# A block's closing steps as a chain of their own beside the next block's row fetches

## The chip, the cores and the metric

The kernel runs on one core of one Trainium2 chip. The time is device microseconds of an execution; the kernel before took 3956.99 us, the median of 3 runs (3949.39 to 3957.73). The profiled execution took 3962.2 us, with a span of 3960.4 us from its first to its last instruction.

## What is computed

One layer of an encoder on 1024 tokens of width 1024: adaLN, a token mixer (attention and a two-way state space model, merged by gates), and then PEER, a channel mixer that picks 128 of 16384 experts for each token. The change lies in the last lines, for the tokens 0 to 383:

```python
def one(xt):                                   # peer, for a block of tokens
    ...                                        # top-k of product keys: idx [T, 8, 16], gates g
    u = u_tab[idx]
    a = jax.nn.gelu(jnp.einsum('thkd,td->thk', u, xt))
    vv = v_tab[idx]
    return jnp.einsum('thk,thkd->td', g * a, vv)
...
x = x + g2[:, None, :] * peer(h, ...)
return rmsnorm(x, final_norm_w)
```

## The kernel before

PEER is done in two ways. **Fetched rows.** For the tokens 0 to 383, three blocks of 128, the rows of `u_tab` and `v_tab` are fetched by index. **Dense.** For the other 640 tokens every expert is computed: the hidden activations of all 16384 experts (`parked_part`, products of three passes at L209 to L211 into the banks `hb`, each followed by a write of the activations `a` to `a_d`), the gates of the chosen experts placed into a dense matrix by one-hot products (`quad` L1478, weighted on GpSimd L1484, products `place` L1493 into a bank, copies to the staging buffers `stg` L1496, in pairs of two 2048 KB writes to `G_d`, L1625), and then, by groups of three experts' rows, `Wh` and `Wl` (L1689, L1692), the splits of `v` (L179, L180), products into banks and `acc` adds on VectorE (L1722). Hidden parts and placement share a stage; the groups, with what is left of the hidden parts, are the dense end behind it.

The fetches run beside that. `fetched()` is a generator; for each block it makes 128 row fetches of `u` (`rows`, L1282: an indirect DMA of GpSimd, one row of 1024 values for each of 128 tokens, into one of ten buffers `br`), and for each of them one row product on VectorE (`dot`, L1314) with the token rows, which `begin` (L1309) has copied into the PSUM tile `gx`. Then come the weights (gelu times gate, transposed), 128 fetches of `v`, and matmuls that sum the rows into `gx` (`add`, L1361). `gx` has two banks and one buffer, so the token rows of the next block, the sums of this one and all that the end below puts there take turns.

The end of a block is `finish` and `final`: copy `gx` to `bacc` (L1369), eight transposes back into `gx` (L1374), load of the residual x1 into the same `bacc` buffer (L1247), eight adds on VectorE (L1252), eight squares on ScalarE (L1260) with sums on PE (L216) into `gx`, the root (`rstd`, L228), its broadcast by PE into `gx` (L237), eight multiplies by the norm's weight (L1271) and the store (L1272). `yield "w"` cuts it into steps.

What sets the order: a planner that keeps three clocks, `at_pe`, `at_dve` and `at_dma`. After each piece of the dense work `feed` (L1503) steps the generator as long as the clock of the DMA lags, 1.6 us for each row; a step that yields "w" ends the round. The instructions of VectorE and GpSimd, and the order of the matmuls in the first stage, are those in which the code is written out; in the dense end PE, ScalarE and SyncE are arranged by the scheduler.

Other single banks come from `P1()`: three `pb` and, behind the placement, `io` as a fourth. The raw weights (`wr`), staging writes, activation writes and the x1 loads all stand in SyncE's queue.

## Time and profile before

| | |
|---|---|
| median of 3 runs | 3956.99 us (3949.39 to 3957.73) |
| profiled execution | 3962.2 us, span 3960.4 us |
| PE (TensorE matmul), busy | 92% |
| PEld (TensorE weight load) | 81% |
| DVE (VectorE) | 65% |
| POOL (GpSimd) | 46% |
| ACT (ScalarE) | 34% |
| DMA, mean over the span | 215 GB/s |
| mean granted clock of TensorE | 0.963 |

A share is a mean over stages. In the span the hidden parts' products begin at 1393 us, the placement's run from 2054 to 2490 us, and the first `Wh` of the dense end is made at 2523 us. The three blocks of fetched rows end at about 2240, 3020 and 3720 us; block 0 ends within the placement, blocks 1 and 2 in the dense end. "SPq" is SyncE's queue of DMA issues. In a timeline the bracket behind a row is the idle time of the engine just before it and what ended it. The clock is given as a share of 2.4 GHz.

### The profile page before, as it was taken

How to read it: one execution, taken by the hardware profiler on the slowest of the kernel's cores; microseconds unless marked ns; L12 is line 12 of the kernel's file. 1: busy time of each engine (PE TensorE's matmuls, PEld its weight loads, DVE VectorE, ACT ScalarE, POOL GpSimd, SP SyncE). 2: the span in 40 equal slices, each digit the busy share in tenths (PEclk: the TensorE clock that was granted, in tenths of full speed). 3: DMA queues.
4: the chain of work that ended last, by engine and by line, in shares of the span. 5: the costliest groups of instructions: out<-in, count | busy, mean ns of one | idle time of the engine just before them, and what ended most of it. 6: DMA issues, size and time to landing. Idle time of an engine off the chain costs nothing. (4 is left out here: it accounts for less than half of the span.)

```text
span 3960.4 us, 61117 instructions
## 1 busy us (share of the span) xinstructions
PE 3631.6 (92%) x22927; PEld 3189.8 (81%) x22927; DVE 2574.5 (65%) x5289; ACT 1356.3 (34%) x2672; POOL 1803.3 (46%) x1526
## 2 busy tenths in 40 slices
PE   7999999988889899999889798699999999999998
PEld 4777767766679799987678698697888999888997
DVE  5788831457672678787875567594447898545556
ACT  5455532223323433322236465222122222222222
POOL 3111122566454567778775456444443444444200
PEclk9999999998899999999999899799999999999999
DMA  5111134233375258877767778888887888888632
GB/s 197 47 46 48 55 117 144 92 106 101 122 241 168 94 201 317 311 284 258 244 231 273 264 265 320 310 300 303 322 323 246 295 297 292 310 317 314 236 117 81
DMA packets 387064, 852.32 MB, mean 215 GB/s; under 512 B 32720, under 2 KB 146896, under 8 KB 384080
## 3 DMA queue, kind: packets, MB, share of 16 engines
q1 hardware_dynamic: 276176, 445.72, 32.9%
q0 software_dynamic: 110592, 402.70, 28.7%
q8 instruction: 180, 2.95, 0.3%
q14 instruction: 116, 0.95, 0.1%
HBM read 739.70 MB, written 108.59 MB: 214 GB/s over the span
## 5 line engine op out<-in xcount | busy, mean ns | idle before, releaser
L209 PE MATMUL hb<-ah,wh 128*128 128x320 f32 x2048 | 653.2, 319 | 24.0 <-ACT a L1459 24.0
L211 PE MATMUL hb<-ah,wl 128*128 128x320 f32 x2048 | 641.1, 313 | 9.7 <-POOL wl L199 9.7
L210 PE MATMUL hb<-al,wh 128*128 128x320 f32 x2048 | 639.9, 312 | 0.0
L1282 POOL DMA_INDIRECT br<-u,bidx x384 | 370.3, 964 | 369.0 <-DVE br L1314 243.2
L199 POOL TENSOR_TENSOR wl<-wr,wh 128x512 fp32r<-128x512 f32 x269 | 352.9, 1317 | 397.3 <-ACT wh L198 367.6
L209 PE MATMUL pb<-Wh,vh 128*128 128x320 f32 x1536 | 477.1, 317 | 57.1 <-ACT Wh L1689 33.7
L180 POOL TENSOR_TENSOR wl<-wr,wh 128x512 fp32r<-128x512 f32 x172 | 233.0, 1358 | 615.5 <-ACT wh L179 450.6
L1282 POOL DMA_INDIRECT br<-v,ixt x384 | 376.8, 981 | 267.5 <-PE gx L1361 155.1
L210 PE MATMUL pb<-Wl,vh 128*128 128x320 f32 x1536 | 481.4, 314 | 1.7 <-DVE Wl L1692 1.6
L211 PE MATMUL pb<-Wh,vl 128*128 128x320 f32 x1536 | 479.6, 313 | 0.0
L1314 DVE SCALAR_TENSOR_TENSOR br<-br,gx 128x1024 f32<-128x1024 f32 x384 | 454.0, 1214 | 8.6 <-DMA br<-u,bidx 6.3
L209 PEld LDWEIGHTS hb<-ah,wh 128*128 128x128 f32 x2048 | 391.9, 191 | 52.7 <-ACT a L1459 28.2
L211 PEld LDWEIGHTS hb<-ah,wl 128*128 128x128 f32 x2048 | 390.7, 191 | 11.3 <-POOL wl L199 10.3
L210 PEld LDWEIGHTS hb<-al,wh 128*128 128x128 f32 x2048 | 391.5, 191 | 0.0
L1722 DVE TENSOR_TENSOR acc<-acc,pb 128x320 f32<-128x320 f32 x491 | 230.6, 485 | 222.2 <-PE pb L211 221.0
L179 ACT CAST vh<-vr 128x512 fp32r<-128x512 f32 x256 | 151.1, 618 | 649.8 <-PE pb L210 449.0
L209 PEld LDWEIGHTS pb<-Wh,vh 128*128 128x128 f32 x1536 | 289.6, 190 | 84.4 <-ACT Wh L1689 37.0
L198 ACT CAST wh<-wr 128x512 fp32r<-128x512 f32 x288 | 178.2, 619 | 397.8 <-PE hb L210 188.2
L210 PEld LDWEIGHTS pb<-Wl,vh 128*128 128x128 f32 x1536 | 292.5, 190 | 5.4 <-DVE Wl L1692 4.3
L211 PEld LDWEIGHTS pb<-Wh,vl 128*128 128x128 f32 x1536 | 292.9, 191 | 0.4
L1478 DVE TENSOR_TENSOR quad<-io,rig 128x1024 f32<-128x1024 f32 x160 | 191.7, 1221 | 139.1 <-PE pb L1493 78.0
L180 DVE TENSOR_TENSOR vl<-vr,vh 128x512 fp32r<-128x512 f32 x256 | 203.9, 797 | 76.8 <-ACT vh L179 76.8
(367 smaller groups left out, 8218.4 us busy)
## 6 DMA issues: line engine op xcount, KB each, us to landing
wr<-uT SPq DMA_DIRECT2D x256, 256.0 KB, 3.9
vr<-v SPq DMA_DIRECT2D x256, 256.0 KB, 5.3
G_d<-stg SPq DMA_DIRECT2D x20, 2048.0 KB, 11.7
gt<-G_d SPq DMA_DIRECT2D x42, 960.0 KB, 6.5
a_d<-a SPq DMA_DIRECT2D x85, 320.0 KB, 5.3
a<-a_d SPq DMA_DIRECT2D x85, 320.0 KB, 5.9
wr<-wi SPq DMA_DIRECT2D x84, 256.0 KB, 2.7
sq<-adaT SPq DMA_DIRECT2D x32, 512.0 KB, 3.8
```

What stands on the lines that cost most here:

```text
L179: ACT.copy(hi, src)
L180: (eng or POOL).tensor_tensor(lo, src, f32(hi), op=OP.subtract)
L198: ACT.copy(h, raw)
L199: late.append(lambda: (eng or POOL).tensor_tensor(w, raw, f32(h), op=OP.subtract))
L209: PE.matmul(o, lhsT=wh, rhs=xh, start=first, stop=False)
L210: PE.matmul(o, lhsT=wh, rhs=xl, start=False, stop=False)
L211: PE.matmul(o, lhsT=wl, rhs=xh, start=False, stop=last)
L1282: POOL.indirect_dma_start(out=r, out_offset=None, in_=A[tab], in_offset=bass.IndirectOffsetOnAxis(ap=idx, axis=0))
L1314: V.scalar_tensor_tensor(v2(r), v2(r), 1.0, hrow[0], op0=OP.mult, op1=OP.mult, accum_out=a[:, s:s + 1])
L1478: V.tensor_tensor(x, iota.unsqueeze(1).unsqueeze(1).to_broadcast([128, 2, 4, 128]), ig[:, 0:2, t:t + 4].unsqueeze(3).to_broadcast([128, 2, ...
L1722: V.tensor_tensor(acc[:, m, js], acc[:, m, js], o, op=OP.add)
```

## The change

The residual, its norm and the store are no longer written out as steps of the generator with "w" between. `finish` copies `gx` to `bacc`, starts the load of the first half of x1, and leaves a generator `tail` behind, with five pieces. `go_on()` runs one piece after every third `u` fetch of the next block; what is left at the end runs in a loop at the end of `fetched`. A piece of the residual makes four transposes into one single bank, four adds in place into `bacc`, and, in the first piece, issues the load of the second half. The halves of x1 share one buffer `bx1` of [128, 4, 128], and the two passes of squares, of [128, 512] each, use it too. Sums and broadcast go to single banks; the norm is made in place. `ba`, the row products' sums, has one buffer instead of two. Lines behind the change are 4 higher (L1314 is L1318, L1282 is L1286, L1484 is L1488, L1722 is L1726), those behind `go_on` more (L1369, the copy, is L1374).

```diff
--- before.py
+++ after.py
@@ -1235,41 +1235,45 @@
         return ig
 
 
-    def final(p, src, t0, n, x1):
-        tl = slice(t0, t0 + n)
-        def of(m):
-            o = src[:, m // 4, m % 4]
-            return o if n == 128 else o.rearrange("p (g i) -> p g i", g=4)[:, :, :n // 4]
-
-        def like(ap):
-            return ap if n == 128 else ap.rearrange("p (g i) -> p g i", g=4)
-
-        nc.sync.dma_start(x1, x1_d[:, :, tl])
-        yield "w"
-        yield "w"
-        yield "w"
+    tails = []
+
+    def half_of(b, k):
+        x = rt.tile([128, 4, 128], F32, name="bx1")
+        nc.sync.dma_start(x, x1_d[:, 4 * k:4 * k + 4, 128 * b:128 * b + 128])
+        return x
+
+    def tail(b, s, x1):
+        for k in range(2):
+            o = P1()
+            for m in range(4):
+                PE.transpose(o[:, 128 * m:128 * m + 128], s[:, 512 * k + 128 * m:512 * k + 128 * m + 128], ident)
+            for m in range(4):
+                V.scalar_tensor_tensor(s[:, 512 * k + 128 * m:512 * k + 128 * m + 128], o[:, 128 * m:128 * m + 128],
+                                       mod[:, 40 + 4 * k + m:41 + 4 * k + m], x1[:, m], op0=OP.mult, op1=OP.add)
+            if k == 0:
+                x1 = half_of(b, 1)
+            yield
+        sq = rt.tile([128, 4, 128], F32, name="bx1")
+        ACT.activation(sq.rearrange("p m t -> p (m t)"), s[:, 0:512], AF.Square)
+        yield
+        o = P1()
+        for k in range(2):
+            if k:
+                sq = rt.tile([128, 4, 128], F32, name="bx1")
+                ACT.activation(sq.rearrange("p m t -> p (m t)"), s[:, 512:1024], AF.Square)
+            for m in range(4):
+                sums(sq[:, m], o, 128, k == 0 and m == 0, k == 1 and m == 3)
+        r = rstd(rt, o, 128, 1.0 / D)
+        yield
+        rb = rbcast(P1(), r, 128)
         for m in range(8):
-            V.scalar_tensor_tensor(like(x1[:, m]), of(m), mod[:, 40 + m:41 + m], like(x1[:, m]), op0=OP.mult, op1=OP.add)
-        yield "w"
-        o = wide()
-        acc = o[:, 0]
-        for m in range(0, 8, 2):
-            some = []
-            for _ in range(2):
-                some.append(p.tile([128, 128], F32, name="fsq", bufs=2)[:, :n])
-                ACT.activation(some[-1], x1[:, m + len(some) - 1], AF.Square)
-            yield "w"
-            for i, sq in enumerate(some):
-                sums(sq, acc, n, m + i == 0, m + i == 7)
-        yield "w"
-        r = rstd(p, acc, n, 1.0 / D)
-        yield "w"
-        yield "w"
-        yield "w"
-        rb = rbcast(o[:, 1], r, n)
-        for m in range(8):
-            V.scalar_tensor_tensor(x1[:, m], x1[:, m], cols[:, C_FN + m:C_FN + m + 1], rb, op0=OP.mult, op1=OP.mult)
-        nc.sync.dma_start(out[:, :, tl], x1)
+            x = s[:, m * 128:m * 128 + 128]
+            V.scalar_tensor_tensor(x, x, cols[:, C_FN + m:C_FN + m + 1], rb, op0=OP.mult, op1=OP.mult)
+        nc.sync.dma_start(out[:, :, 128 * b:128 * b + 128], s.rearrange("p (m t) -> p m t", m=8))
+
+    def go_on():
+        if tails and next(tails[0], 0) == 0:
+            tails.pop(0)
 
     def fetched():
         zb = [rt.tile([128, 4, 160], F32, name=f"zb{i}") for i in range(2)]
@@ -1289,7 +1293,7 @@
 
         for b in range(NB):
             assert b in ready
-            a = rt.tile([128, 128], F32, name="ba", bufs=2)
+            a = rt.tile([128, 128], F32, name="ba")
             ixt = rt.tile([128, 128], I32, name="ixt", bufs=2)
             aT = rt.tile([128, 128], F32, name="aT")
             yield from drain(NROW - 1 - SLACK)
@@ -1344,6 +1348,8 @@
                 if s == slots - 32:
                     flipped()
                 yield "u"
+                if s % 3 == 2:
+                    go_on()
             ahead.append((0, weights_of))
             acc = []
 
@@ -1363,17 +1369,12 @@
                 return
                 yield
 
-            def finish(b=b, acc=acc, n=4 * steps):
+            def finish(b=b, acc=acc):
                 s = rt.tile([128, D], F32, name="bacc")
-                yield "w"
                 ACT.copy(v2(s), acc[0])
-                yield "w"
-                yield "w"
-                o = wide().rearrange("p s (m t) -> p s m t", m=4)
-                for m in range(8):
-                    PE.transpose(o[:, m // 4, m % 4], s[:, m * 128:(m + 1) * 128], ident)
-                x1 = rt.tile([128, 1024], F32, name="bacc")[:, :8 * n].rearrange("p (m t) -> p m t", m=8)
-                yield from final(rt, o, b * 128, n, x1)
+                tails.append(tail(b, s, half_of(b, 0)))
+                return
+                yield
 
             for i in range(steps):
                 R = []
@@ -1386,6 +1387,9 @@
         yield from drain(0)
         while ahead:
             yield from ahead.pop(0)[1]()
+        while tails:
+            go_on()
+            yield "w"
 
     fetch = fetched()
 
```

Three places of the engines' orders follow, first as they were and then as they are.

**GpSimd, at the end of block 0**, in the placement (`wl` is the low half of a weight tile of the hidden parts, `quad` the weighting of a placement, `br<-u` a row fetch). Before:

```order
L199 TENSOR_TENSOR wl<-wr,wh 128x512
L1484 TENSOR_TENSOR quad<-quad,rig 128x512 x2
L1282 DMA br<-u,bidx 128x1024 x15
L199 TENSOR_TENSOR wl<-wr,wh 128x512 x6
L1484 TENSOR_TENSOR quad<-quad,rig 128x512 x2
```

With the change:

```order
L1286 DMA br_19938<-u,bidx_7888 128x1024
L199 TENSOR_TENSOR wl_19963<-wr_19960,wh_19962 128x512
L1488 TENSOR_TENSOR quad_20012<-quad_20012,rig_17839 128x512
L1286 DMA br_20028<-u,bidx_7888 128x1024
L1286 DMA br_20038<-u,bidx_7888 128x1024
L1286 DMA br_20040<-u,bidx_7888 128x1024
L199 TENSOR_TENSOR wl_20010<-wr_20007,wh_20009 128x512
L199 TENSOR_TENSOR wl_20079<-wr_20076,wh_20078 128x512
L1488 TENSOR_TENSOR quad_20025<-quad_20025,rig_17839 128x512
L1488 TENSOR_TENSOR quad_20138<-quad_20138,rig_17839 128x512
L1286 DMA br_20154<-u,bidx_7888 128x1024
L1286 DMA br_20156<-u,bidx_7888 128x1024
```

The fifteen fetches in a row, with six weight splits behind them, are now spread in twos and threes between splits and weightings.

**SyncE, at the end of block 0** (`wr` is the load of raw weights, `a_d` the write of hidden activations, `G_d` that of the placed gates, `x_d` the source of x1). Before:

```order
L190 DMA wr<-uT 128x512
L1625 DMA G_d<-stg 128x4096 x2
L1247 DMA bacc<-x_d 128x8x128
L190 DMA wr<-uT 128x512
L1472 DMA a_d<-a 128x640
L1272 DMA out<-bacc 1024x1x128
```

With the change:

```order
L1629 DMA G_d<-stg 128x4096 x2
L1242 DMA bx_20318<-x_d 128x4x128
L1476 DMA a_d<-a 128x640
L190 DMA wr<-uT 128x512 x4
L1476 DMA a_d<-a 128x640
L190 DMA wr<-uT 128x512 x2
```

The load behind the staging pair is now the second half of x1 alone; the first half is issued further ahead, among the query weights.

**VectorE, at the end of block 1**, in the dense end (L1314 and, with the change, L1318 are the row products; L1722 and L1726 the `acc` adds; L180 the low half of a `v` tile). Before:

```order
L1722 TENSOR_TENSOR acc<-acc,io 128x320
L1722 TENSOR_TENSOR acc<-acc,pb 128x320
L1271 SCALAR_TENSOR_TENSOR bacc<-bacc,cols,gx 128x128 x8
L1314 SCALAR_TENSOR_TENSOR br,ba<-br,gx 128x1024 x12
L1722 TENSOR_TENSOR acc<-acc,pb 128x320 x2
L180 TENSOR_TENSOR vl_28003<-vr,vh_28002 128x512
```

With the change:

```order
L1318 SCALAR_TENSOR_TENSOR br,ba<-br,gx 128x1024
L1726 TENSOR_TENSOR acc<-acc,pb 128x320 x2
L180 TENSOR_TENSOR vl_27573<-vr,vh_27572 128x512
L1251 SCALAR_TENSOR_TENSOR bacc<-io,mod,bx_27517 128x128 x4
L1318 SCALAR_TENSOR_TENSOR br,ba<-br,gx 128x1024 x2
L1726 TENSOR_TENSOR acc<-acc,pb 128x320 x2
L180 TENSOR_TENSOR vl_27618<-vr,vh_27617 128x512
L1318 SCALAR_TENSOR_TENSOR br,ba<-br,gx 128x1024
L1726 TENSOR_TENSOR acc<-acc,pb 128x320
L1726 TENSOR_TENSOR acc<-acc,io 128x320
L1251 SCALAR_TENSOR_TENSOR bacc<-pb,mod,bx_27585 128x128 x4
```

The twelve products that followed each other stand apart, between the adds of the residual and the `acc` adds.

## Rows read from the trace of the kernel before

**Rows 1.** The page: the span, and part 1, engine, busy us, share of the span, instructions.

```profile
span 3960.4 us, 61117 instructions
...
PE 3631.6 (92%) x22927; PEld 3189.8 (81%) x22927; DVE 2574.5 (65%) x5289; ACT 1356.3 (34%) x2672; POOL 1803.3 (46%) x1526
```

**Rows 2.** Busy time by stretch: from and to, length, then busy us of PE, PEld, VectorE (DVE), ScalarE (ACT) and GpSimd (POOL) with the number of instructions, mean granted clock of PE as a share of 2.4 GHz, share of the DMA engines, GB/s. The end of block 0, the placement behind it, the end of block 1, the stretch behind it, the end of block 2.

```profile
2190.00:2290.00 100.00, 77.02 (x590) 72.41 (x589) 47.95 (x74) 44.73 (x121) 47.36 (x45) 0.88 0.67 241
2290.00:2450.00 160.00, 150.06 (x1102) 149.08 (x1101) 115.61 (x141) 96.22 (x285) 102.48 (x97) 0.97 0.78 283
3000.00:3100.00 100.00, 88.50 (x617) 85.70 (x616) 82.06 (x154) 26.66 (x49) 36.97 (x36) 0.93 0.79 271
3100.00:3400.00 300.00, 281.12 (x1853) 274.49 (x1851) 261.25 (x470) 72.47 (x127) 124.79 (x120) 0.99 0.87 293
3700.00:3760.00 60.00, 59.86 (x463) 55.34 (x463) 36.76 (x76) 20.48 (x38) 5.17 (x4) 1.00 0.57 188
```

**Rows 3.** The list of waits, PE alone, 2190 to 2290 us: who waited for whom, us in total, times, longest.

```profile
PE gx L216 <- DVE bacc L1252: 10.6, 1, 10.6
PE hb L211 <- POOL wl L199: 9.1, 1, 9.1
PE hb L209 <- ACT a L1459: 1.4, 1, 1.4
PE gx L237 <- DVE rstd L228: 1.4, 1, 1.4
PE gx L216 <- ACT fsq L1260: 0.5, 1, 0.5
```

**Rows 4.** Timeline around the end of block 0, by engine (SyncE's queue, VectorE, PE): start us, us, engine, line, operation, out<-in, how many in the row, and in brackets the idle time before it and what ended it. A row with xN is N instructions that follow each other.

```profile
2223.19 0.89 SPq L1625 DMA_DIRECT2D G_d<-stg  x2
2226.19 0.52 SPq L1247 DMA_DIRECT2D bacc<-x_d  x1
...
2237.99 2.16 DVE L1252 SCALAR_TENSOR_TENSOR bacc<-gx,mod,bacc 128x128 f32<-128x128 f32 x8 [9.61 <-DMA bacc<-x_d]
...
2240.30 0.44 PE L216 MATMUL gx<-fsq,ka 128*32 128x32 f32 x16 [10.58 <-DVE bacc L1252]
2240.67 2.08 PE L1493 MATMUL pb<-quad 128*128 128x128 f32 x8
...
2245.42 0.31 PE L211 MATMUL hb<-ah,wl 128*128 128x320 f32 x1
...
2248.20 1.16 PE L1493 MATMUL pb<-quad 128*128 128x128 f32 x8
...
2249.34 0.31 PE L210 MATMUL hb<-al,wh 128*128 128x320 f32 x1
...
2250.80 0.31 PE L211 MATMUL hb<-ah,wl 128*128 128x320 f32 x1
```

**Rows 5.** Timeline behind the end of block 0: GpSimd's first row fetch behind the new `gx` and its first weight split behind the fetches, then PE.

```profile
2257.96 0.94 POOL L1282 DMA_INDIRECT br<-u,bidx  x1 [5.14 <-ACT gx L1309]
...
2274.06 3.73 POOL L199 TENSOR_TENSOR wl<-wr,wh 128x512 fp32r<-128x512 f32 x3
...
2275.39 0.64 PE L211 MATMUL hb<-ah,wl 128*128 128x320 f32 x1 [9.12 <-POOL wl L199]
2275.83 0.47 PE L209 MATMUL hb<-ah,wh 128*128 128x320 f32 x1
...
2279.52 0.30 PE L211 MATMUL hb<-ah,wl 128*128 128x320 f32 x1
```

**Rows 6.** Timeline at the end of block 1: VectorE (the row products, then the `acc` adds), then PE.

```profile
3031.39 1.22 DVE L1314 SCALAR_TENSOR_TENSOR br<-br,gx 128x1024 f32<-128x1024 f32 x1 [1.14 <-ACT gx L1309]
...
3043.95 1.22 DVE L1314 SCALAR_TENSOR_TENSOR br<-br,gx 128x1024 f32<-128x1024 f32 x1
...
3045.09 0.88 DVE L1722 TENSOR_TENSOR acc<-acc,pb 128x320 f32<-128x320 f32 x2
...
3045.63 0.64 PE L209 MATMUL pb<-Wh,vh 128*128 128x320 f32 x1 [5.35 <-DVE acc L1722]
...
3050.33 0.47 PE L211 MATMUL pb<-Wh,vl 128*128 128x320 f32 x1
...
3053.61 0.41 PE L209 MATMUL pb<-Wh,vh 128*128 128x320 f32 x1 [1.84 <-DVE acc L1722]
...
3057.12 0.63 PE L209 MATMUL io<-Wh,vh 128*128 128x320 f32 x1 [2.08 <-ACT Wh L1689]
```

**Rows 7.** Timeline of ScalarE at the end of block 0: two pairs of squares with their gaps, and a pass over [128, 512].

```profile
2240.74 0.51 ACT L1260 ACTIVATE fsq<-bacc 128x128 f32<-128x128 f32 x2 [1.80 <-PE gx L216]
...
2246.85 0.51 ACT L1260 ACTIVATE fsq<-bacc 128x128 f32<-128x128 f32 x2 [0.25 <-PE gx L216]
...
2258.83 0.62 ACT L198 CAST wh<-wr 128x512 fp32r<-128x512 f32 x1 [1.14 <-PE hb L210]
```

**Rows 8.** The list of waits: of PE in 2290 to 2450 us; and, for the end of the placement, the row of PE in 2450 to 2560 us.

```profile
PE pb L1493 <- ACT stg L1496: 9.9, 4, 3.4
...
PE pb L209 <- ACT Wh L1689: 24.5, 3, 21.1
```

**Rows 9.** DMA issues by line: out<-in, queue, operation, how many, KB each, median us from issue to landing. The staging writes are from the page's part 6, the residual load from the whole list.

```profile
G_d<-stg SPq DMA_DIRECT2D x20, 2048.0 KB, 11.7
...
bacc<-x_d SPq DMA_DIRECT2D x3, 512.0 KB, 4.2
```

## The prediction

> **What bounds the kernel now.** The share of each engine comes first [rows 1]: TensorE (PE) is busy for 92% of 3960.4 us, VectorE (DVE) for 65%. That is a mean over stages, so the next view is the busy time by stretch [rows 2]. Two stretches stand out, the ends of block 0 (2190 to 2290 us) and of block 1 (3000 to 3100 us): PE is busy for 77.0 and 88.5 of 100 us, at a mean granted clock of 0.88 and 0.93, where the stretches just behind have 150.1 of 160 us at 0.97 and 281.1 of 300 us at 0.99. At the end of block 2 (3700 to 3760 us) PE is busy for 59.9 of 60 us. So the diff can win at two of its three places and only lose at the third.
>
> What PE waits for at the end of block 0 stands in the list of waits [rows 3]: 23.0 us in five waits. The timeline shows two causes. The first is the residual [rows 4]. SyncE issues the load of x1 at 2226.19, about 3 us behind the write of a staging pair (2 x 2048 KB, from 2223.19; the size stands in [rows 9]). VectorE begins the adds at 2237.99, 11.8 us after the issue and after 9.61 us idle, and PE, whose next instruction is the row sums of the squares, stands for 10.58 us. The second is a catch-up [rows 5]. The planner has stepped through the waits "w" of the old end without fetching, and then takes 15 rows in a row: the last 13 keep GpSimd busy from 2257.96 to 2274.06, the low half of a weight tile (`wl`) is behind them on the same engine, and PE stands for 9.12 us for it. After each long stand the records show PE at the lower of its two levels: matmuls of 0.47 us instead of 0.31, and a step of 0.146 us (10 steps from 2249.34 to 2250.80) becomes 0.275 (15 from 2275.39 to 2279.52).
>
> At the end of block 1 only the second cause is there, and on another engine [rows 6]: the row products wait for `gx`, which the old end holds, until 3031.39; twelve then run back to back on VectorE, the `acc` adds behind them start at 3045.09, and PE, out of banks, waits 5.35 us, again followed by 18 matmuls at the lower level (3045.63 to 3050.33).
>
> **The change, part by part.** The order of the instructions moves in three windows only; ahead of, between and behind them the engines' orders agree but for line numbers and one load, the first residual half of block 0, which SyncE now issues among the query weights, 800 us early. No PE matmul is added or removed, so all that can change is waiting.
>
> *Block 0, removed.* The waits of [rows 3], 23.0 us, lose their causes: the sums no longer stand behind a load issued one step before, `gx` is given back after one copy, no step is a "w", and the run of 15 rows becomes runs of two and three. Slow matmuls go with them: 8 + 12 after the first stand (2240.67 to 2245.42, 4.75 us where 8 + 12 take 2.6 at the pace of 2248.20 to 2250.80) and 15 steps after the second (4.1 us where 0.146 each makes 2.2) [rows 4, 5]: 2.1 + 1.9 = 4.0 us. Together 27.0 us.
>
> *Block 0, added.* (a) Both square passes use the one buffer `bx1`, and PE has the two groups of sums back to back: the second square waits for the first sums, the second sums for it. A [128, 512] pass of ScalarE takes 0.62 us and the gap before such a pass 0.25 [rows 7]; with another 0.25 on the way back that is 1.1, and I take 1.3 us. Bounds: 1.1, and 1.8 (the gap before the second pair of squares) with it, 2.9. (b) The transposes now take one of the three banks that the placement uses, and keep it until four adds are done; at this point the staging copies wait for the pair's write. The nearest row is PE's wait for such copies, 9.9 us in four, longest 3.4 [rows 8]. Between 0 and 3.4 I take 1.5, since two placements stand between the pair and the transposes. (c) The second residual half can be loaded only when the first four adds have freed `bx1`, and it stands behind the same staging pair on SyncE. I reckon it issued some 8 us behind the pair instead of 3; if the pair's bytes set the landing, as 14.8 us from 2223.19 to 2237.99 suggest, it comes 7 us later, and VectorE has three quads and three row products to do until then, some 8 us at PE's pace. I take 0; bounds 0 and 9.6 (the wait of before, unchanged). (d) With the stalls gone, the ordinary waits of the placement appear: 9.9 us in 160 [rows 8], 6.2% of the 73 us that remain, 4.5 us. Sum: 27.0 - 1.3 - 1.5 - 0 - 4.5 = **19.7 us**; bounds 27.0 - 2.9 - 3.4 - 9.6 - 4.5 = 7 and 27.0 - 1.1 = 26.
>
> *Block 1.* Removed: 5.35 us, 2.2 us of slow matmuls (17 steps in 4.70 us instead of 2.5), and of the waits of 1.84 and 2.08 us just behind, which the backlog feeds, about half: 2.0. Added: the ordinary waits of a stretch with row products, 18.9 us in 300 [rows 2], 6.3% of 50 us or 3.2; the squares, 0.7 since five matmuls stand between the sums; VectorE's wait for the second half, 1.0, with three row products, four adds and a split as cover; and its wait for the square root's table, now loaded behind the squares instead of well ahead, 1.0. Net 9.55 - 5.9 = 3.65, **4 us**; bounds 0 (the load late by 4.2, the median of the old one [rows 9]) and 8.
>
> *Block 2.* PE was full, so nothing is won. Between the two groups of adds stand only two `acc` adds, one per 1.32 us of PE, 2.6 us, and the second half needs about 4.2 [rows 9]. VectorE is late by 1.6 us plus its issue of 0.5; three free banks cover most, and I take 1.4, and 0.6 for the squares: **-2 us**; bounds 0 and -6 (nothing covers).
>
> *Free.* That early load of 256 KB; eighteen fewer square passes of 0.3 us on ScalarE, which is idle for two thirds of the span; the adds in place; `ba` with one buffer, whose last reader is over long before the next block's first product.
>
> Sum: 19.7 + 4 - 2 = 22 us. The profiled execution took 3962.2 us and would take 3940; the median of the runs lies 5.2 us below it, so the forecast is 3957 - 22 = **3935 us**. Can the gain get lost downstream? Behind window 0 the orders are equal, and the next long stand, 24.5 us of PE for the first `Wh` [rows 8], follows the last staging write, so it moves along.
>
> **The rivals.**
> *The second half is late everywhere.* For it: x1 took 11.8 us from issue to use in block 0, and the diff issues half of it later than before. Against it: 4.2 us is the median, and work stands between. It decides where VectorE comes to the fifth add before the landing. Then block 0 keeps 9.6 us and the slow matmuls behind it (2.1), block 1 loses its 4 and block 2 another 3: a gain of 22 - 18.7, **3954 us**. Beside it the Trainium skill ("DMA: Bandwidth & Descriptors", section "Rules for kernel authors") has a rule against such a load: issue early, work, wait late; one buffer lets the diff do that for the first half alone, and the 9.61 us of [rows 4] agree with what the rule fears. The same page of the Trainium skill (section "Anatomy of one DMA") gives about 2.0 us plus bytes over 436 GB/s, for 256 KB an estimate of 2.6 us; by that the load would hide at every end, and the sum would be 2 us better; the trace's 4.2 and 11.8 us are above it.
> *The gain is given back at the end of the placement.* If the 24.5 us stand were set by something that doesn't move, only blocks 1 and 2 would count: 3957 - 2 = **3955 us**. Against it: the writes it follows are behind the placements on the same engines.
> *Slower: SyncE is held.* In all three ends SyncE stands at the second half until four adds free the buffer, and the weight loads queue behind. If that lasts longer than PE takes for the three raw halves of weights in stock (3 x 24 matmuls x 0.146 = 10.5 us), PE starves as in [rows 5], 9.1 + 1.9 us at each end: 33 us against the 22 won, **3968 us**. Against it: I reckon 8 us of holding in block 0 and less later.
>
> **How the numbers follow.** Two runs of this kernel are told apart from about 0.2%, 8 us. The forecast gets 0.82, the late half 0.07, the gain given back 0.06, the held queue 0.05. The forecast's own range, by the bounds that seem open, is 3926 to 3946. All bounds at once give 22 as 1 to 34 us; the range that leaves out 2 in 10 or less takes the upper bounds whole, 3921, and goes up to 3950, short of the two rivals of no change. Faster by over 0.2%: the forecast, 0.82. Within 0.2%: the first two rivals, 0.13. Slower: the third, 0.05.
>
> **What would show it.** In the changed profile the longest run of row fetches at 2200 to 2300 us is gone, and PE's waits for `wl` and for the residual add there with it; no twelve row products in a row near 3030 us; three waits of PE of about 1 us at the sums for `bx1`. The last row fetches and the last stage come some 22 us earlier. I am wrong if VectorE waits several us for `bx1` from the DMA, if PE waits long for staging copies around the transposes, or if the stand before the first `Wh` grows by what the placement won.

## The result

The changed kernel took 3935.9 us, the median of 5 runs (3930.39 to 3940.41), against 3956.99 of the kernel before in the same session (5 runs, 3949.39 to 3959.29): a ratio of 0.9939, 95% interval [0.9919, 0.9959]. Two more sessions, on two different chips, gave 0.9922 [0.9909, 0.9935] and 0.9952 [0.9934, 0.9970]. Ratios are taken from fast runs alone, and one run of e_b0 below, 6742 us at a granted clock of 0.505, is left out as slow. Forecast were 3935 us, and a gain of 22 us in parts of 19.7, 4 and -2 us at the ends of blocks 0, 1 and 2.

### The profile page after: what moved, and what is told of

Read it like the earlier page. It is cut to its first block, busy times and chain, and to the rows that moved or that the text cites. A ratio compares the mean times of both kernels' runs of the same rounds, so it can differ in the third digit from the quotient of the medians.

```text
span 3938.6 us, 61081 instructions
## 1 busy us (share of the span) xinstructions
PE 3626.7 (92%) x22927; PEld 3185.6 (81%) x22927; DVE 2579.0 (65%) x5289; ACT 1353.3 (34%) x2654; POOL 1808.9 (46%) x1526
## 4 chain that ended last, share of the span: by engine, by line
PE 33%; DMA 8%; DVE 7%; ACT 2%; issue 2%; POOL 1%; SPq 0%; ACTq 0%; DVEq 0%; POOLq 0%
PE pb L209 4%; PE pb L210 4%; PE pb L211 4%; DMA vr<-v 4%; PE gx L1367 4%; PE hb L209 3%; PE pb L1497 3%; PE hb L210 3%; PE hb L211 3%; DVE br L1318 2%; DMA G_d<-stg 2%; PE io L209 1%; PE io L210 1%; PE io L211 1%; DVE acc L1726 1%
## 5 line engine op out<-in xcount | busy, mean ns | idle before, releaser
L209 PE MATMUL hb<-ah,wh 128*128 128x320 f32 x2048 | 653.2, 319 | 21.7 <-ACT a L1463 21.7
L1286 POOL DMA_INDIRECT br<-u,bidx x384 | 372.4, 970 | 366.6 <-DVE br L1318 259.7
L209 PE MATMUL pb<-Wh,vh 128*128 128x320 f32 x1536 | 476.8, 317 | 49.5 <-ACT Wh L1693 32.4
L180 POOL TENSOR_TENSOR wl<-wr,wh 128x512 fp32r<-128x512 f32 x172 | 233.6, 1362 | 619.7 <-ACT wh L179 455.9
L1286 POOL DMA_INDIRECT br<-v,ixt x384 | 377.2, 982 | 270.2 <-PE gx L1367 161.5
L1318 DVE SCALAR_TENSOR_TENSOR br<-br,gx 128x1024 f32<-128x1024 f32 x384 | 454.9, 1213 | 5.3 <-DMA br<-u,bidx 5.3
L209 PEld LDWEIGHTS hb<-ah,wh 128*128 128x128 f32 x2048 | 392.3, 192 | 51.0 <-ACT a L1463 25.9
L1726 DVE TENSOR_TENSOR acc<-acc,pb 128x320 f32<-128x320 f32 x491 | 230.1, 485 | 207.2 <-PE pb L211 205.3
L209 PEld LDWEIGHTS pb<-Wh,vh 128*128 128x128 f32 x1536 | 289.6, 190 | 76.3 <-ACT Wh L1693 36.2
L180 DVE TENSOR_TENSOR vl<-vr,vh 128x512 fp32r<-128x512 f32 x256 | 208.2, 813 | 79.4 <-ACT vh L179 79.3
## 6 DMA issues: line engine op xcount, KB each, us to landing
G_d<-stg SPq DMA_DIRECT2D x20, 2048.0 KB, 12.9
```

The lines of the kernel that those rows point to most:

```text
L180: (eng or POOL).tensor_tensor(lo, src, f32(hi), op=OP.subtract)
L209: PE.matmul(o, lhsT=wh, rhs=xh, start=first, stop=False)
L1286: POOL.indirect_dma_start(out=r, out_offset=None, in_=A[tab], in_offset=bass.IndirectOffsetOnAxis(ap=idx, axis=0))
L1318: V.scalar_tensor_tensor(v2(r), v2(r), 1.0, hrow[0], op0=OP.mult, op1=OP.mult, accum_out=a[:, s:s + 1])
L1726: V.tensor_tensor(acc[:, m, js], acc[:, m, js], o, op=OP.add)
```

## The profile after

The page, span and part 1, against [rows 1]:

```profile
span 3938.6 us, 61081 instructions
...
PE 3626.7 (92%) x22927; PEld 3185.6 (81%) x22927; DVE 2579.0 (65%) x5289; ACT 1353.3 (34%) x2654; POOL 1808.9 (46%) x1526
```

PE's busy time fell by 5 us and the span by 22: most of what went was waiting. Busy time by stretch, columns as in [rows 2]; the last stretch is the end of block 2, some 20 us earlier than before:

```profile
2190.00:2290.00 100.00, 90.42 (x709) 86.68 (x709) 59.35 (x83) 58.01 (x160) 54.44 (x52) 0.95 0.77 273
2290.00:2450.00 160.00, 149.61 (x1096) 148.24 (x1095) 120.05 (x155) 90.27 (x265) 104.99 (x100) 0.98 0.85 307
3000.00:3100.00 100.00, 91.72 (x648) 89.53 (x647) 85.98 (x160) 25.60 (x43) 38.35 (x37) 0.95 0.86 281
3680.00:3740.00 60.00, 58.77 (x459) 57.74 (x458) 37.46 (x76) 17.80 (x30) 6.82 (x4) 1.00 0.48 159
```

In the first row PE has 90.4 us of 100 and a granted clock of 0.95, where [rows 2] have 77.0 and 0.88. The third has 91.7 against 88.5. Block 2 was full before and is no longer quite full: 58.8 of 60 us.

PE's waits from 2180 to 2300 us, as in [rows 3]:

```profile
PE pb L1497 <- ACT stg L1500: 14.2, 3, 5.6
PE pb L216 <- ACT bx L1263: 1.0, 1, 1.0
```

None of the five waits of [rows 3] is there. In their place stand waits for staging copies (4.0 and 4.6 us; the longest of the three, 5.6 us at 2186, lies ahead of the change and has its like in the trace of before, 5.4 us at 2188) and a wait of 1.0 us at the sums, as term (a) had it.

SyncE's queue at the end of block 0, against [rows 4], and its waits from 2200 to 2310 us:

```profile
2221.81 0.83 SPq L1629 DMA_DIRECT2D G_d<-stg  x2
2230.84 0.37 SPq L1242 DMA_DIRECT2D bx<-x_d  x1
```

```profile
SPq L1242 <- DVE bacc L1251: 8.2, 1, 8.2
...
SPq L1242 <- PE pb L216: 4.7, 1, 4.7
```

The second half is issued 9.0 us behind the staging pair (2221.81 to 2230.84), because the queue stood for 8.2 us until four adds had freed the buffer. It stood once more, for 4.7 us, at the first half for block 1 (issued at 2267.18), until the sums had read the squares out of the same buffer. Who suffered from it is told by VectorE (three rows) and PE (two):

```profile
2229.70 1.12 DVE L1251 SCALAR_TENSOR_TENSOR bacc<-pb,mod,bx 128x128 f32<-128x128 f32 x4
2244.73 1.21 DVE L1318 SCALAR_TENSOR_TENSOR br<-br,gx 128x1024 f32<-128x1024 f32 x1
2245.87 1.12 DVE L1251 SCALAR_TENSOR_TENSOR bacc<-pb,mod,bx 128x128 f32<-128x128 f32 x4
...
2266.54 0.46 PE L216 MATMUL pb<-bx,ka 128*32 128x32 f32 x32 [0.97 <-ACT bx L1263]
...
2285.90 2.08 PE L1497 MATMUL pb<-quad 128*128 128x128 f32 x8 [4.61 <-ACT stg L1500]
```

VectorE passes from a row product at 2244.73 straight to the second four adds at 2245.87, with no idle time before them: the half had come in the 15 us since its issue. PE's stands from 2200 to 2300 us are 4.0 us for staging copies (at 2233), 0.97 at the sums and 4.61 for staging copies again.

Block 1, against [rows 6]. VectorE, then PE:

```profile
2978.10 1.22 DVE L1318 SCALAR_TENSOR_TENSOR br<-br,gx 128x1024 f32<-128x1024 f32 x1
...
2981.34 1.12 DVE L1251 SCALAR_TENSOR_TENSOR bacc<-io,mod,bx 128x128 f32<-128x128 f32 x4
...
2989.78 1.11 DVE L1251 SCALAR_TENSOR_TENSOR bacc<-pb,mod,bx 128x128 f32<-128x128 f32 x4
...
3008.62 0.82 DVE L1690 TENSOR_TENSOR a<-a,gt 128x640 f32<-128x640 f32 x1 [5.08 <-DMA gt<-G_d]
...
3013.84 0.66 PE L216 MATMUL io<-bx,ka 128*32 128x32 f32 x32 [4.95 <-DVE acc L1726]
```

The row products begin at 2978.10, among the `acc` adds, and not in a run of twelve behind the end; PE stood 17.7 us earlier in its work here than in the trace of before, so this is 36 us sooner than the 3031.39 of [rows 6]. New is the wait of 5.08 us for the gates (`gt`), behind which PE stands 4.95 us at the sums (3.6 and 1.1 us in the other two traces of the changed kernel).

Block 2, VectorE (two rows) and PE:

```profile
3681.18 1.12 DVE L1251 SCALAR_TENSOR_TENSOR bacc<-pb,mod,bx 128x128 f32<-128x128 f32 x4 [3.47 <-PE pb L1249]
...
3687.12 1.13 DVE L1251 SCALAR_TENSOR_TENSOR bacc<-pb,mod,bx 128x128 f32<-128x128 f32 x4 [3.82 <-DMA bx<-x_d]
...
3688.30 0.41 PE L209 MATMUL pb<-Wh,vh 128*128 128x320 f32 x1 [1.24 <-DVE bacc L1251]
```

Here the second half is late, as forecast: 3.82 us of VectorE, of which 1.24 reach PE.

## Where the time went, stage by stage

Runs of one kernel in one session lie 10 to 28 us apart (the kernel before: 3949 to 3959 in the first session, 3953 to 3981 in that of e_b0), and its medians by session go from 3957 to 3974, so the traces are compared by stages. The placement runs from the first to the last of its 1280 products. The row for it in the trace of before, and of the change (least, median and longest ns of one, first and last start):

```profile
L1493 PE MATMUL pb<-quad x1280: 272/276/583, 2053.9 to 2490.1; 128*128 128x128 f32 x183
```

```profile
L1497 PE MATMUL pb<-quad x1280: 270/275/583, 2050.7 to 2469.9; 128*128 128x128 f32 x183
```

That is 436.2 and 419.2 us. But most of the placement has nothing to do with the change, and scatters: its products from the 961st to the 1121st, which no edit touches, took 54.2 to 59.4 us over all traces, with before_again at the one end and the changed kernel at the other. So block 0 is read from the products around the change alone, from the start of the 561st to that of the 801st (2195.5 to 2311.8 us in the trace of before, 116.3 us; 2194.3 to 2292.9 in that of the change, 98.6 us). For blocks 1 and 2 the marks are products of L209, which all these kernels have 5616 times: in order of start, from the 3764th to the 4181st (2990.32 to 3205.10 in the trace of before, 214.8 us) and from the 4999th to the 5229th (3640.17 to 3760.40, 120.2 us).

| kernel | placement | block 0: products 561 to 801 | block 1 | block 2 | whole, ratio to before in its session |
|---|---|---|---|---|---|
| before | 436.2 | 116.3 | 214.8 | 120.2 | |
| before_again | 434.1 | 116.2 | 213.5 | 120.0 | |
| the change | 419.2 | 98.6 | 207.2 | 120.4 | 0.9939 [0.9919, 0.9959] |
| after_again | 418.9 | 98.3 | 209.8 | 122.4 | 0.9922 [0.9909, 0.9935] |
| after_third | 415.1 | 101.5 | 206.0 | 123.3 | 0.9952 [0.9934, 0.9970] |
| e_b0 (chain in block 0 only) | 423.0 | 102.0 | 214.4 | 120.6 | 0.9958 [0.9944, 0.9972] |
| e_b12 (chain in blocks 1, 2 only) | 439.7 | 117.0 | 205.7 | 121.4 | 0.9986 [0.9973, 0.9999] |
| e_load (before, x1 early) | 431.0 | 108.1 | 213.6 | 120.4 | 0.9976 [0.9960, 0.9992] |
| e_cap (before, rounds capped) | 419.9 | 103.5 | 214.0 | 120.1 | 0.9967 [0.9954, 0.9979] |
| e_both (both edits) | 412.4 | 95.6 | 215.5 | 120.7 | 0.9934 [0.9916, 0.9952] |
| e_w14 (change with its w back) | 432.0 | 111.5 | 214.2 | 118.8 | 0.9977 [0.9966, 0.9987] |
| e_two (change, x1 whole) | 414.8 | 98.2 | 204.3 | 119.9 | 0.9946 [0.9934, 0.9959] |
| e_two_again | 423.9 | 101.8 | 205.0 | 120.4 | 0.9943 [0.9925, 0.9961] |
| e_mix (e_both in block 0, chain in 1, 2) | 415.7 | 95.1 | 208.7 | 122.0 | 0.9935 [0.9921, 0.9949] |

Block 0: with the old end 116.2, 116.3 and 117.0 us, mean 116.5; with the chain 98.3, 98.6, 101.5 and 102.0, mean 100.1: **16.4 us**. Block 1: 213.5, 214.4 and 214.8 against 205.7, 206.0, 207.2, 208.7 and 209.8, means 214.2 and 207.5: **6.7 us**. Block 2: 120.0, 120.2 and 120.6 against 120.4 to 123.3, means 120.3 and 121.9: **-1.6 us**. Sum 21.5. Traces of one kernel differ by up to 4 us in each of these stretches.

## The experiments

**The chain in block 0 alone, and in blocks 1 and 2 alone.** Both ends are in the kernel, and the block decides:

```diff
-            ahead.append((0, finish))
+            ahead.append((0, finish if b in (0,) else finish_old))
```

(`(1, 2)` in the second.)

> The new chain for block 0 alone; the ends of blocks 1 and 2 are as before (their squares share the buffer bx1 in pairs, ba has one buffer). Theory (each end's waits are lost where they stood, and nothing is given back): the last placement product comes about 17 us earlier than before, as in the changed kernel (20.2 less the 3.2 us by which that run was ahead at its first placement product), and the whole is 16 to 18 us faster, about 3940. Rival (the placement's gain is mostly given back at the first Wh, and the time is won in block 1): at most 8 us faster, over 3949.

> The new chain for blocks 1 and 2 alone; block 0 ends as before. Theory: 7.5 us in block 1 (PE's lag between 2990 and 3205 us in the changed kernel's trace) and none in block 2, about 3950; PE's two stands of about 10 us behind the end of block 0 are there as before. Rival (as above): 12 us or more, under 3945. Third: the new ends cost at block 2 what they win at block 1, 3957.

Measured were 0.9958 and 0.9986 of 3971.1 us, or 16.7 and 5.6 us. In the table the first changes block 0 alone (102.0 us against 116.5), the second block 1, and block 2 by 1 us. The parts add up to the whole, and what the placement wins is kept to the end: the rival by which the gain is given back at its end has fallen.

**The two stands of block 0, each by itself.** One kernel loads x1 early and keeps everything else of before; the other caps the catch-up (its "f" is what the steps of `finish` and `final` yield in place of "w").

```diff
+                x1 = rg.tile([128, D], F32, name="br", bufs=NROW).rearrange("p (m t) -> p m t", m=8)
+                nc.sync.dma_start(x1, x1_d[:, :, 128 * b:128 * b + 128])
                 s = rt.tile([128, D], F32, name="bacc")
                 yield "w"
...
-                x1 = rt.tile([128, 1024], F32, name="bacc")[:, :8 * n].rearrange("p (m t) -> p m t", m=8)
...
-        nc.sync.dma_start(x1, x1_d[:, :, tl])
```

```diff
         while at_dma < max(at_pe, at_dve):
+            if behind and got == 2:
+                return
+            got += 1
             kind = step_fetch()
+            if kind == "f":
+                behind = True
+                break
...
+        else:
+            behind = False
```

> The kernel before with one edit: x1 is loaded whole into a row buffer at the start of finish, ahead of the staging pair, so that the adds do not wait for it; the waits w, the long hold of gx and the run of 15 row fetches stay. Theory (two causes that add up): PE's wait of 10.6 us at the sums goes, with 2 us of slow matmuls; the wait of 9.1 us for wl stays; 10 to 13 us faster in the placement, about 3946. Rival (the two waits hide each other: what the first releases the next bank or weight tile takes): the wait for wl or for staging copies grows by about what the load gave, under 4 us won, over 3953.

> The kernel before with one edit: after a step of an end the planner takes at most two rows in a round until its clock has caught up, so that neither the 15 row fetches of block 0 nor the twelve row products of block 1 stand in a row; the load of x1, the waits w and the hold of gx stay. Theory: the wait of 9.1 us for wl goes with about 2 us of slow matmuls, and in block 1 the wait of 5.35 us at the acc adds and half of what follows; the load's 10.6 us stay; 14 to 18 us faster, about 3941. Rival (what wins is that gx is given back early; a capped round leaves the rows as late as before): under 4 us, over 3953.

For measure, the kernel before once more:

> The kernel before once more, for a trace from the same chip as the three runs beside it. Theory: PE's waits of about 10.6 us (residual) and 9.1 us (wl) at the end of block 0 and of 5.4 us behind the end of block 1 come again within 0.5 us, since they follow from the order; what the clock does in the last 40 us (granted 0.86 and 0.59 in the two traces at hand) need not.

Its waits came again at 11.1, 7.6 (1.5 us off) and 5.4 us.

PE's waits between the 561st and the 801st product, first of before_again (2191.3 to 2307.6 us), then of e_load (2196.5 to 2304.6), then of e_cap (2191.0 to 2294.6):

```profile
PE gx L216 <- DVE bacc L1252: 11.1, 1, 11.1
PE hb L211 <- POOL wl L199: 7.6, 1, 7.6
PE pb L1493 <- ACT stg L1496: 1.9, 1, 1.9
```

```profile
PE hb L211 <- POOL wl L199: 9.1, 1, 9.1
PE pb L1493 <- ACT stg L1496: 3.0, 2, 1.9
...
PE gx L216 <- DVE br L1251: 0.9, 1, 0.9
```

```profile
PE gx L216 <- DVE bacc L1252: 10.9, 1, 10.9
PE pb L1493 <- ACT stg L1496: 1.4, 1, 1.4
```

Each edit takes away its own wait and leaves the other as it was: 11.1 becomes 0.9 with the early load, while wl keeps its 9.1; with the cap the wl wait is gone and the load's stays at 10.9. So both causes were read rightly. The early load won 8.4 us in block 0 (108.1 against 116.5), a little less than the 10 to 13 expected: the waits for staging copies grew by 1.1 us only, but all of PE's waits there fell by 8 to 9 us in sum, and the 2 us of slow matmuls were not saved beside that. The cap won 13.0 us (103.5), just under the 14 to 18 expected. The whole times agree (0.9976 and 0.9967 of 3971.1 us are 9.5 and 13.1 us), though their intervals overlap and do not by themselves tell the two apart.

In block 1 the cap won nothing (214.0), where 5 us or more were expected. PE's waits from 2965 to 3070 us in e_cap have

```profile
PE pb L209 <- DVE acc L1732: 4.9, 1, 4.9
```

against 5.35 us in [rows 6], although no more than three row products stand together in VectorE's order there. So the run of twelve was not the cause.

**Do the two stands add up?**

> The kernel before with the edits of e_load and e_cap together; w, gx and the old steps of the end stay. So far the placement, from its first to its last product, took 434 to 440 us with the old end, 419 to 423 with the new one, 431 with the early load alone and 420 with the capped round alone. Theory A (the two stands add up): 414 to 416 us. Theory B (the writes of the staging pairs set the pace behind the two stands; the wait for x1 lies beside one for staging copies): 418 to 421, as with the capped round alone, and PE's waits for staging copies between 2150 and 2310 us grow from 6.8 us to 11 or more. In both, block 1 takes 213 to 215 us between the same products as before (207 to 210 with the change), since its row products still come behind the end. Whole: A 0.9945, B 0.996 of before.

They do: block 0 takes 95.6 us, 20.9 less than before, where the two edits alone make 8.4 + 13.0 = 21.4; the placement takes 412.4. Block 1 is again unmoved (215.5). Theory B's sign, 11 us or more of staging waits between 2150 and 2310 us, came too:

```profile
PE pb L1493 <- ACT stg L1496: 11.5, 4, 5.3
```

But it says nothing here. Between fixed times a kernel that runs elsewhere in time has other waits: of the 11.5 us, 3.8 end at 2150, just within, and their like in e_cap ends at 2148, just outside. PE's waits between the 561st and the 801st product, in e_both (2192.8 to 2288.4 us) and then in after_again (2198.2 to 2296.6):

```profile
PE pb L1493 <- ACT stg L1496: 2.4, 2, 1.3
...
PE gx L216 <- DVE br L1251: 0.9, 1, 0.9
```

```profile
PE pb L1497 <- ACT stg L1500: 8.6, 2, 4.4
PE pb L216 <- ACT bx L1263: 1.0, 1, 1.0
```

With the same causes removed, the old end in `gx` has 2.4 us of staging waits and the chain 8.6: 6.2 us. So it is in every trace: 8.1 to 9.2 us in the seven with the chain at block 0, 1.4 to 3.0 in the seven with the old end there. The chain's transposes and sums take banks that the placement's products use, the old end's do not. This is the price of term (b), if nothing else in the chain's place in the orders makes the difference; the runs do not isolate it.

**The change with its waits back.** Fourteen steps "w" behind `finish`, all else as changed:

```diff
                 tails.append(tail(b, s, half_of(b, 0)))
-                return
-                yield
+                for _ in range(14):
+                    yield "w"
```

> The changed kernel with one part undone: fourteen steps w behind finish, so that the planner again passes fourteen rounds without fetching and then takes twelve rows in a row; the chain, its banks and its early halves stay, and all its pieces now come within that run. Theory (the run of fetches and products is what costs, whatever banks the end uses): PE waits 7 to 9 us for wl in block 0 again and about 5 us for banks in block 1, and the close pieces add some us of their own; 14 to 20 us slower than the changed kernel, 0 to 8 faster than before. Rival (the banks of gx and the residual's load are what count): within 5 us of the changed kernel.

> The changed kernel once more. Theory: 19 to 23 us faster than before on this chip (ratio 0.994 to 0.9955), PE's lead over the kernel before on the same chip grows by 15 to 17 us between 2155 and 2500 us and by 6 to 8 between 2990 and 3205, and not at the end of block 2. If the last stage's loss of 3.3 us in the first trace belongs to the change, its TensorE clock there is again about 0.6 where the kernel before has 0.86; if it is a matter of the execution, the two can stand the other way.

The placement falls back to 432.0 us, block 0's stretch to 111.5 and block 1 to 214.2: all of block 1's gain and 11.4 of the 16.4 us of block 0 hang on the steps "w", with the chain and its banks kept. The whole is 0.9977 where after_again on the same chip is 0.9922, some 22 us, a little over the range. The place was not the expected one. PE's waits between the 561st and the 801st product in e_w14 (2199.2 to 2310.8 us), and VectorE's adds of the two halves:

```profile
PE pb L216 <- ACT bx L1257: 9.4, 1, 9.4
PE pb L1497 <- ACT stg L1500: 8.6, 2, 4.5
```

```profile
2246.84 1.12 DVE L1251 SCALAR_TENSOR_TENSOR bacc<-pb,mod,bx 128x128 f32<-128x128 f32 x4
...
2254.45 1.12 DVE L1251 SCALAR_TENSOR_TENSOR bacc<-pb,mod,bx 128x128 f32<-128x128 f32 x4 [3.08 <-DMA bx<-x_d]
```

PE waits 9.4 us for the first squares and not for wl. The squares use the buffer of the halves and come behind the second four adds, and these wait 3.08 us for the second half, which is issued behind the first four. In the changed kernel 15 us lie between its issue and its adds; here it is issued at 2247.98, and 6.5 us with three row products do not cover it. By the trace this is the late half, the prediction's rival, at block 0; a version of e_w14 with x1 whole, which would test it, was not run.

In block 1 `gx` is given back as early as in the changed kernel, and no more than six row products stand together. But the first of them starts 32.6 us behind the mark of block 1 (the 3764th product of L209). It is 41 us in before, e_cap and e_both, which win nothing there, and 5 to 6 us wherever the chain ends block 1 as changed.

**Both halves at once.** x1 whole in a row buffer when `finish` runs, the squares as changed:

```diff
-                tails.append(tail(b, s, half_of(b, 0)))
+                x1 = rg.tile([128, D], F32, name="br", bufs=NROW).rearrange("p (m t) -> p m t", m=8)
+                nc.sync.dma_start(x1, x1_d[:, :, 128 * b:128 * b + 128])
+                tails.append(tail(b, s, x1))
```

> The changed kernel with x1 loaded whole into a row buffer when finish runs, so that no half waits for the adds and SyncE never stands at the second half. Theory: little hangs on the second half: VectorE's wait of 3.8 us at block 2 goes and PE's of 1.2 us with it, the gates' load of block 1 is issued some us earlier and takes part of PE's 4.9 us there; 1 to 5 us faster than the changed kernel. Rival (late half: the single buffer costs what the trace doesn't name): 8 us or more faster. Rival (the row buffer that it takes from the fetches costs more): slower than the changed kernel.

> The version with x1 whole in a row buffer again, beside the changed kernel on the same chip. In its trace it had block 0, 1 and 2 faster than the changed kernel by 2, 3 and 1 us, while the median of its runs was 7 us slower. Theory (the stages are faster, the median was the scatter of few runs): 2 to 7 us faster than the changed kernel. Rival (the row buffer taken from the fetches costs in most executions): 3 to 8 us slower.

> The changed kernel as the measure for the version above: 17 to 29 us faster than before (ratio 0.9925 to 0.9955).

Block 2 goes back to 119.9 and 120.4 us, where six traces with the old end have 120.0 to 120.7: its loss goes with the late half. Block 0's stretch is as in the changed kernel (98.2 and 101.8). Block 1 is at 204.3 and 205.0, 2 to 3 us better. The stand at the sums of block 1 stays, since PE's waits from 2965 to 3070 us in e_two have

```profile
PE io L216 <- DVE acc L1721: 3.7, 1, 3.7
```

and VectorE again waits for the gates just before it, so the late gates are not the half's doing; what orders that load is open. In time the version is not told apart from the changed kernel: 0.9946 against 0.9922 on one chip, 0.9943 against 0.9952 on the other, and the stages gained are smaller than that scatter. Neither theory is settled by that.

**Put together.** The early load and the cap as above, and the block decides:

```diff
-            ahead.append((0, finish))
+            ahead.append((0, finish if b else finish_old))
```

> What the runs point to, put together: block 0 by the old steps in gx with the residual loaded early and the rounds capped (412 us for the placement, 415 to 419 with the change), blocks 1 and 2 by the new chain (206 to 210 us for block 1, 213 to 215 with the old end). Theory (the stages are independent of each other): placement 412 to 415 us, block 1 206 to 209, block 2 as with the change; 25 to 31 us faster than before, ratio 0.992 to 0.9937, some 5 us better than the changed kernel. Rival (the placement's lead is lost on the way to block 1, or the old end's late rows make block 1 end otherwise): no better than the changed kernel, 0.994 or more.

The placement took 415.7 us, block 1 208.7, and the ratio is 0.9935: the stages came within a microsecond of what was expected, but the whole is within what the changed kernel itself shows (0.9922 to 0.9952). Block 0's stretch took 95.1 us, close to e_both's 95.6, and PE's waits for staging copies between its products (2202.4 to 2297.5 us) are short as there:

```profile
PE pb L1546 <- ACT stg L1549: 1.9, 2, 1.1
```

Block 0 is thus some 5 us shorter with the two small edits than with the chain, but in the whole time no version here is shown to beat the changed kernel.

## Why the prediction was right, point by point

*The reading.* Two stretches with room, one without: so it was. No work was removed, the waits and the slow matmuls behind them were the gain, and nothing was lost downstream.

*Block 0: 19.7 forecast, 16.4 measured.* The five waits of [rows 3] went entirely. All of PE's waits between the 561st and the 801st product sum to 24.1 to 25.2 us with the old end and 9.6 to 11.8 with the chain, some 14 us; the other 2.4 of the gain are what is left for slow matmuls, where 4.0 were forecast. Term (a), 1.3 us: 1.0 in two traces, 3.1 in after_third and e_b0, just over its bound. (The gap of 0.25 us in it is that before a pair of small squares; the [128, 512] pass of [rows 7] has 1.14.) Term (c), 0 us with an issue 8 us behind the pair: the issue came 9.0 us behind, and nobody waited. Terms (b) and (d) together, 1.5 + 4.5 = 6.0 us: the staging waits are 8.6 us where before has 1.9, so 6.7. The sum was right and its parts were not. With the stalls gone and the banks as before, in e_both, these waits are 2.4 us: the ordinary waits (d) cost 0.5 us and not 4.5, and up to 6.2 are (b), over its bound of 3.4. The row from which (b) was bounded showed what the placement's copies cost when nobody else takes a bank.

*Block 1: 4 forecast, 6.7 measured, within its bounds of 0 to 8.* The step that failed is its cause. I counted the wait behind twelve row products in a row; e_cap and e_both take the run apart and win nothing. What the kernels without the gain have in common is the late start of the row products, 33 to 41 us behind the mark where the changed kernel has 5. e_w14 brings back the late start, but neither the held `gx` nor the run of twelve, and loses all of the 6.7. That the late products then fill VectorE just when the `acc` adds need it is read from its order and was not tried by itself. I also did not see the wait for the gates (4.95, 3.6 and 1.1 us of PE in three traces), which takes part of the gain.

*Block 2: -2 forecast, -1.6 measured.* VectorE is late by 3.82 us (2.1 forecast) and PE by 1.24 (1.4 forecast), and with x1 whole the loss is gone. But the changed kernel's traces go from 120.4 to 123.3 us, so the size is not known to better than a microsecond or two; in after_again PE has no wait for the half at all, but 1.35 us for a row of `v`.

*The signs.* The runs of fetches and products and both long waits are gone, and the last stage comes earlier by 25 us. Of the three waits of about 1 us at the sums, block 0 alone has one. Two signs of being wrong came, both small: VectorE's 3.82 us for `bx1` at block 2, and 4.0 and 4.6 us of PE for staging copies around the transposes. The upper bounds taken whole give 3957 - 34 = 3923 and not 3921.

*The rivals.* In the changed kernel the late half is there at block 2 alone; in e_w14, where the pieces come close together, its trace has it at block 0 too. The gain is not given back: e_b0 keeps it. SyncE did stand, for 8.2 and 4.7 us in block 0, but PE did not starve: it has no wait for a weight tile there. By the prediction's reckoning the three raw halves in stock last 10.5 us; whether a longer stand would have starved it was not tried. The Trainium skill's rule against a load issued late ("DMA: Bandwidth & Descriptors", section "Rules for kernel authors") is borne out where nothing covers the load (3.82 us of VectorE at block 2) and not where other work does. The 2.6 us that the prediction worked out for a half come from a section of the Trainium skill ("DMA: Bandwidth & Descriptors", section "Anatomy of one DMA") on transfers issued from GpSimd; these are issued from SyncE, and the six landed in 4.1 to 4.7 us.

*Luck.* That 3935 and 3935.9 agree so closely is in part chance: the other two sessions gave gains of 29 and 16 us by their medians, block 0 won 3 us less than forecast and block 1 almost as much more, and within block 0 the errors of (b) and (d) cancel.

## What to carry to other kernels

When a planner steps through waits without doing work, look for what it does afterwards: the catch-up was worth more (13.0 us) than the visible stall beside it (8.4 us), though the trace listed the stall as the longer wait. Take one stand away at a time. Compare stages and lists of waits between the same instructions, not between the same times: from 2150 to 2310 us PE's staging waits are 8.9 us in before and 12.3 in e_load, between the same products 1.9 and 3.0. When work moves into banks that a saturated stage shares, price it by who waits for those banks, not by its own length.

## What the runs showed of the chip beside that

The last 40 us hold the same instructions in every kernel, but not the same time. PE's granted clock from the first broadcast of the last norm to the last products behind it, in before, in the changed kernel, and in e_b12 (columns as above):

```profile
3934.40:3947.00 12.60, 11.34 (x100) 9.01 (x100) 6.73 (x15) 2.96 (x7) 0.00 (x0) 0.86 0.30 105
```

```profile
3909.00:3925.50 16.50, 14.98 (x100) 11.12 (x100) 6.93 (x15) 2.96 (x7) 0.00 (x0) 0.59 0.23 80
```

```profile
3941.00:3956.00 15.00, 14.34 (x91) 11.33 (x91) 6.33 (x13) 2.96 (x7) 0.00 (x0) 0.55 0.25 89
```

From that broadcast's first product to the last product of L209 it took 10.9, 14.3 and 14.5 us; after_again, the changed kernel again, took 11.3. PE has waited 2.86 us just before the broadcast in both of the first two. In before its matmuls take 0.47 us at first and 0.31 from 3938 us on, 4 us behind the broadcast; in the changed kernel they take 0.47, the pace of the lower of the two levels (1.2 GHz), from 3911 to 3922 us. After_again has the short time, so the same kernel shows both times, and the change does not fix which. Whether it makes the long one more frequent is open: five of the eight traces with the chain at block 2 have 14.3 to 14.6 us, none of the six with the old end there (10.5 to 12.9). In the first trace the 3.4 us hide that the 5547th product of L209 came 25.4 us earlier than before (3874.9 against 3900.3 us), where the span is 21.8 us shorter.
